# Hyena layer: the first x1 products ahead of the first convolution, half of the output rows by token halves, norms without GpSimd

## The chip, the cores and the metric

The kernel runs on one core of a Trainium2 chip. The metric is the device time of one execution in microseconds (us); lower is better. The engines are named as in the profile: PE (TensorE), DVE (VectorE), ACT (ScalarE), POOL (GpSimd) and SP (SyncE, which here only issues DMAs).

## What is computed

A trunk of two layers over 512 latent tokens of width 1024 with 256 context tokens, all in fp32. Layer 0 is attention and an MLP, layer 1 a Hyena mixer and an MLP, each behind a modulated RMSNorm. What matters here:

```python
def rmsnorm(x, g):
    y = x * lax.rsqrt(jnp.mean(x * x, axis=-1, keepdims=True) + EPS)
    return y * g

def modulate(x, g, shift, scale):
    return rmsnorm(x, g) * (1 + scale) + shift

def hyena_mixer(h, ...):
    z = short_conv(h @ w_in, conv_w, conv_b)     # 3 taps along the tokens
    x1, x2, v = jnp.split(z, 3, axis=-1)         # 1024 columns each
    y = v
    for n, gate in enumerate((x1, x2)):
        y = gate * bidir_long_conv(y, hf[:, n], hb[:, n], skip[n])   # over all 512 tokens
    return y @ w_out

x = x + g1 * hyena_mixer(modulate(x, norm1_g, sh1, sc1), ...)
x = x + g2 * sq_relu_mlp(modulate(x, norm2_g, sh2, sc2), w1, w2)
```

## The kernel before

The stream x is kept transposed as `xT`: 8 tiles of 128 features by 512 tokens. A product of near fp32 precision is made of three fp32r matmuls (`mm3`, L107): high by high, high by low, low by high. So every weight tile is split by `split_w` (L119) into `whi` (a cast on ACT) and `wlo` (a subtraction on DVE, or on POOL where `lo_eng` says so), and every operand `h` into `h_hi` and `h_lo`. Raw weights come through the two `wraw` buffers, loaded by SP; the split ones lie in two buffers `whi` and two `wlo`. PE, ACT, DVE and POOL each run their own list of instructions in order. The kernel's source gives the order in which work is stated; the Tile framework's planner makes the list of each engine from it and sets the waits.

A norm (`normT`, L409) works on one half of the tokens (256 columns). `inv_rms` (L394) squares the 8 tiles on ACT (`nsq`), lets POOL add up seven of them in `nacc` (L404), and sums over the partitions by fp32 products with ones (L405, L406). After the reciprocal root (ACT, then a Newton step on DVE) each of the 8 tiles is scaled on DVE (`nxr`, L418) and shifted to `h_hi` on ACT (L420); `h_lo` is made on DVE for even tiles (L426), and for odd ones by a second copy on ACT (L423) and a subtraction on POOL (L424). In the Hyena layer's finish these tiles lie in re-used ones, which the profile names `U` and `y`.

`project_norm_project` (L839) joins two stages by token halves A and B: the projection of half A (8 steps of 128 features), some steps of half B (`ahead`), the norm of A, the rest of B, then the first two tiles of the next product on half A, the norm of B, and those two on half B. It stands in three places: from attention to MLP 0, from MLP 0 to the Hyena layer, and from the Hyena layer to MLP 1. `add_proj_steps` (L816) makes the projection: for each pair of output tiles a weight load and split, and for each tile `kt` times `mm3` and an eviction on DVE that adds to `xT` (L835). With `kept` the split weights of half A stay for half B.

The Hyena layer (`hyena`, L1111) works on four blocks c of 256 channels. `project` (L1129) makes one of v, x1, x2 of a block in two steps, each 24 matmuls of 512 columns and the short convolution (`shorts`, L1116: three ACT evictions, four POOL additions). For each block `conv1` transposes v, makes a spectrum on PE (L948), multiplies it with a filter on DVE and prepares the inverse (`P`); `gate1` (L1168) is the inverse product on PE times x1 on DVE; then a second `hyena_conv`, whose result (`E`, `O`) goes through `gate2` (L1180) into rows 2c and 2c+1 of Y, split into `yhi` and `ylo`. Between these, `fill(n)` (L1213) takes n steps of independent products from the chain `other`, which hold PE busy while DVE works on a convolution:

```python
        other = chain(P_(0, "x1"), P_(1, "v"), P_(0, "x2"), P_(1, "x1"), P_(2, "v"), P_(1, "x2"), P_(2, "x1"), P_(3, "v"),
                      P_(2, "x2"), P_(3, "x1"), wo(0, 2), P_(3, "x2"), wo(2, 6))
        R1 = conv1(0)
        fill(4)
        for c in range(4):
            u = gate1(c, R1, turn_x1(c))
            R2 = self.hyena_conv(hp, Tf, u, load_k(1, c), False)
            if c < 3:
                R1 = conv1(c + 1)
            fill((3, 3, 3, 8)[c])
            gate2(c, R2)
            fill((3, 3, 9, 0)[c])
```

`wo(r0, r1)` is the product of rows r0 to r1-1 of Y with w_out, 8 steps (one per output tile); its low halves are made on POOL. Rows 0 to 5 are done in the loop, at 512 columns. Rows 6 and 7 are done in `finish` (L1376), by token halves through `project_norm_project`, with the split weights kept in tiles that the layer no longer needs.

Of the kernel before, what the change touches and what calls it, by code (L numbers as in the profile page):

```python
# [12 lines left out]
ALU = mybir.AluOpType  # L13
# [40 lines left out]
class Parts:  # L54


    def __init__(self, whole, rest, parts):
        self.whole, self.rest, self.turns = whole, rest, {n: cycle(i) for n, i in parts.items()}

    def tile(self, shape, dtype, name):  # L60
        if name in self.turns:
            return self.whole[:, next(self.turns[name])]
        return self.rest.tile(shape, dtype, name)


def f(ap):
    return ap.bitcast(F32)


class Kernel:  # L70
# [323 lines left out]
    def inv_rms(self, np_, cols):  # L394
# [4 lines left out]
        acc = np_.tile([P, n], F32, name="nacc")  # L399
        for k in range(KD):  # L400
            s = acc if k == 0 else np_.tile([P, n], F32, name="nsq")
            nc.scalar.activation(out=s, in_=self.xT[:, k, cols], func=AF.Square)
            if 0 < k < KD - 1:
                nc.gpsimd.tensor_tensor(out=acc, in0=acc, in1=s, op=ALU.add)  # L404
        nc.tensor.matmul(ps, self.ones, acc, start=True, stop=False)  # L405
        nc.tensor.matmul(ps, self.ones, s, start=False, stop=True)  # L406
        return self.rsqrt_bcast(np_, ps, n, 1.0 / D, "n")

    def normT(self, np_, h, gcol, shcol, cols):  # L409
# [5 lines left out]
        for k in range(KD):  # L415
# [5 lines left out]
            if k % 2:  # L421
                u = np_.tile([P, n], F32, name="nu")
                nc.scalar.activation(out=u, in_=t, func=AF.Identity, bias=sh)  # L423
                nc.gpsimd.tensor_tensor(out=lo, in0=u, in1=f(hi), op=ALU.subtract)  # L424
            else:
                nc.vector.scalar_tensor_tensor(out=lo, in0=t, scalar=sh, in1=f(hi), op0=ALU.add, op1=ALU.subtract)  # L426
# [684 lines left out]
    def hyena(self, h, zp, first, open_hp, kdram, gcol, finish):  # L1111
# [84 lines left out]
        def load_k(n, c):  # L1196
# [4 lines left out]
        wo = lambda r0, r1, cols=slice(0, S), kept=None: self.add_proj_steps(  # L1201
            w_out, list(range(r0, r1)), gcol, lambda k: Y[r0 + k], cols, kept, (nc.gpsimd, nc.gpsimd))
        Z[0] = {"v": []}
        for m in range(2):
            shorts(0, "v", 2048, m, first[m])
        hp = open_hp()
        Tf, Ti = self.load_tables(hp, True)
        P_ = lambda c, *nms: project(c, [(nm, {"v": 2048, "x1": 0, "x2": 1024}[nm]) for nm in nms])


        other = chain(P_(0, "x1"), P_(1, "v"), P_(0, "x2"), P_(1, "x1"), P_(2, "v"), P_(1, "x2"), P_(2, "x1"), P_(3, "v"),
                      P_(2, "x2"), P_(3, "x1"), wo(0, 2), P_(3, "x2"), wo(2, 6))
# [281 lines left out]
```

## Time and profile before

| | |
|---|---|
| three runs | 1565.3, 1568.7, 1571.17 us; median 1568.7 |
| the profiled execution | 1564.55 us, its span 1562.8 us |
| mean granted clock of PE | 0.976 of full speed |
| busy, share of the span | PE 93%, PE's weight loads 76%, DVE 71%, ACT 45%, POOL 26% |

Times in the trace are in us from the span's start. A matmul's row shows when it starts and how long it lasts until its result is there; matmuls overlap, so the rate of a stream is the distance of two starts, not the length of one. In brackets stands how long the engine was idle before the instruction, and what released it. The Hyena layer's first v product and the norm before it end at about 907 us, the layer's products by token halves begin at about 1167, and the MLP of layer 1 runs at full width from about 1210 to the end.

### The profile page before, as it was taken

The numbers are of one execution on the slowest core, as the hardware profiler recorded it, in microseconds if no ns is written. First come the engines' busy times: TensorE is split into PE (matmuls) and PEld (weight loads), VectorE is DVE, ScalarE is ACT, GpSimd is POOL, SyncE is SP. The second block draws the span as 40 slices with busy tenths as digits, with TensorE's granted clock in tenths as the row PEclk, the third lists the DMA queues.
The fourth block names the chain that finished last, engine by engine and source line by source line (L and its number), as shares of the span: only waits on it lengthen the run. The fifth ranks groups of instructions, "written<-read, shape, count | busy, mean of one in ns | idle before, by whom it ended". The sixth has DMA issues, their size and how long they took to land. (4 is left out here: it accounts for less than half of the span.)

```text
span 1562.8 us, 19761 instructions
## 1 busy us (share of the span) xinstructions
PE 1449.0 (93%) x7468; PEld 1192.0 (76%) x7468; DVE 1109.5 (71%) x1582; ACT 699.7 (45%) x1140; POOL 403.1 (26%) x340
## 2 busy tenths in 40 slices
PE   8688899999989999989999979999987999999998
PEld 2356588888877777878789967788776888888898
DVE  3898899887688988898765659798847434344454
ACT  3534587766653344344425444434325413232242
POOL 0440235232320322232220345445354000000001
PEclk9899999999999999999999989999998999999999
DMA  8557200221346655564334323231222223233241
GB/s 314 196 176 224 48 1 21 59 53 50 109 157 232 202 191 175 175 198 159 121 108 162 110 86 106 84 108 41 95 91 72 81 81 108 87 102 104 85 135 55
DMA packets 134461, 186.06 MB, mean 119 GB/s; under 512 B 16584, under 2 KB 117709, under 8 KB 131294
## 3 DMA queue, kind: packets, MB, share of 16 engines
q1 hardware_dynamic: 132192, 174.62, 34.6%
q0 software_dynamic: 1440, 9.70, 1.8%
q8 instruction: 59, 0.97, 0.3%
q10 hardware_dynamic: 734, 0.48, 0.1%
q14 instruction: 36, 0.29, 0.1%
HBM read 171.67 MB, written 10.49 MB: 117 GB/s over the span
## 5 line engine op out<-in xcount | busy, mean ns | idle before, releaser
L125 ACT CAST whi<-wraw 128x1024 fp32r<-128x1024 f32 (+3 forms) x211 | 198.9, 949 | 360.4 <-PE sm L110 341.1
L126 DVE TENSOR_TENSOR wlo<-wraw,whi 128x1024 fp32r<-128x1024 f32 (+2 forms) x195 | 241.4, 1242 | 105.8 <-ACT whi L125 95.8
L110 PE MATMUL sm<-h_lo,whi 128*128 128x512 f32 (+1 forms) x720 | 275.6, 384 | 3.9 <-POOL h_lo L424 3.1
L109 PE MATMUL sm<-h_hi,whi 128*128 128x512 f32 (+1 forms) x720 | 276.4, 387 | 2.2 <-ACT h_hi L420 2.2
L111 PE MATMUL sm<-h_hi,wlo 128*128 128x512 f32 (+1 forms) x720 | 274.1, 382 | 3.6 <-DVE wlo L126 3.6
L110 PE MATMUL sm<-mHlo,whi 128*128 128x512 f32 (+1 forms) x640 | 223.5, 349 | 6.0 <-DVE mHlo L172 6.0
L109 PE MATMUL sm<-mHhi,whi 128*128 128x512 f32 (+1 forms) x640 | 225.9, 353 | 0.5 <-ACT whi L125 0.3
L111 PE MATMUL sm<-mHhi,wlo 128*128 128x512 f32 (+1 forms) x640 | 223.2, 349 | 1.9 <-DVE wlo L126 1.9
L835 DVE SCALAR_TENSOR_TENSOR xT<-sm,mod,xT 128x512 f32<-128x512 f32 (+1 forms) x136 | 83.7, 621 | 150.7 <-PE sm L111 150.5
L110 PEld LDWEIGHTS sm<-h_lo,whi 128*128 128x128 f32 x720 | 136.0, 189 | 32.9 <-POOL h_lo L424 5.5
L111 PEld LDWEIGHTS sm<-h_hi,wlo 128*128 128x128 f32 x720 | 135.8, 189 | 32.1 <-DVE wlo L126 6.1
L109 PEld LDWEIGHTS sm<-h_hi,whi 128*128 128x128 f32 x720 | 134.8, 189 | 30.7 <-ACT h_hi L420 2.8
L110 PEld LDWEIGHTS sm<-mHlo,whi 128*128 128x128 f32 x640 | 121.7, 190 | 22.5 <-DVE mHlo L172 7.0
L111 PEld LDWEIGHTS sm<-mHhi,wlo 128*128 128x128 f32 x640 | 121.5, 190 | 18.7 <-DVE wlo L126 3.4
L109 PEld LDWEIGHTS sm<-mHhi,whi 128*128 128x128 f32 x640 | 121.4, 190 | 18.2 <-issue 1.7
L929 POOL TENSOR_TENSOR Kout<-kE,kO 128x512 f32<-128x512 f32 x32 | 46.3, 1471 | 264.6 <-DVE kE L1065 264.6
L370 DVE SCALAR_TENSOR_TENSOR modacc<-modw,silu,modacc 128x1024 f32<-128x1024 f32 x63 | 84.1, 1335 | 27.4 <-DMA modw<-in_w_mod 27.2
L1126 POOL TENSOR_TENSOR zx<-zx,zt 128x384 f32<-128x384 f32 x64 | 79.4, 1260 | 93.1 <-ACT zt L1124 91.8
L639 POOL TENSOR_SCALAR prob<-prob,smx 128x768 f32<-128x768 f32 x64 | 60.4, 943 | 146.9 <-DVE smx L638 91.8
L1245 POOL TENSOR_TENSOR facc<-facc,fsq 128x256 f32<-128x256 f32 x12 | 9.5, 790 | 333.1 <-ACT fsq L1243 333.1
L169 ACT CAST mHhi<-ms 128x512 fp32r<-128x512 f32 x64 | 39.6, 620 | 79.8 <-DVE ms L875 79.5
L637 ACT ACTIVATE prob<-big,smx,qry 128x768 f32<-128x768 f32 x64 | 63.7, 997 | 11.8 <-DVE smx L635 11.2
(458 smaller groups left out, 3002.4 us busy)
## 6 DMA issues: line engine op xcount, KB each, us to landing
wraw<-in_mlp_w SPq DMA_DIRECT2D x67, 1024.0 KB
modw<-in_w_mod SPq DMA_DIRECT2D x80, 512.0 KB
wraw<-in_h_w_in SPq DMA_DIRECT2D x12, 1024.0 KB
wm<-in_w_mod SPq DMA_DIRECT2D x8, 1024.0 KB
kd<-Kout POOLq DMA_DIRECT2D x8, 1024.0 KB, 5.4
Kin<-kd SPq DMA_DIRECT2D x8, 1024.0 KB
wraw<-in_a_w_in SPq DMA_DIRECT2D x5, 1024.0 KB
wraw<-in_a_w_out SPq DMA_DIRECT2D x9, 512.0 KB
```

Source lines behind the costliest of these rows:

```text
L109: mm(ps, w.hi, x.hi, start=first, stop=False)
L110: mm(ps, w.hi, x.lo, start=False, stop=False)
L111: mm(ps, w.lo, x.hi, start=False, stop=last)
L125: nc.scalar.copy(hi, r3)
L126: (lo_eng or nc.vector).tensor_tensor(out=lo, in0=r3, in1=f(hi), op=ALU.subtract)
L169: nc.scalar.copy(dst.hi, src)
L370: nc.vector.scalar_tensor_tensor(out=acc, in0=w, scalar=s, in1=acc, op0=ALU.mult, op1=ALU.add)
L637: nc.scalar.activation(out=p, in_=sf, func=AF.Exp, bias=sm[:, 1:2], scale=sc, accum_out=sm[:, 2:3])
L639: nc.gpsimd.tensor_scalar(out=p, in0=p, scalar1=sm[:, 3:4], scalar2=1.0, op0=ALU.mult, op1=ALU.mult)
L835: nc.vector.scalar_tensor_tensor(out=xt, in0=ps, scalar=gcol[:, d:d + 1], in1=xt, op0=ALU.mult, op1=ALU.add)
L929: tt = lambda e, o, x, y, op: e.tensor_tensor(out=o, in0=x, in1=y, op=op)
L1126: nc.gpsimd.tensor_tensor(out=t[:, o0:o0 + n], in0=t[:, o0:o0 + n], in1=b[:, i0:i0 + n], op=ALU.add)
```

## The change

- The two products of x1 of block 0 are stated ahead of the tables, of the first convolution and of everything else in the block loop; the chain `other` starts with v of block 1, so that each `fill` takes steps that lie one pair later.
- In the loop only rows 0 to 3 of Y go through w_out (8 steps of 12 matmuls, five ahead of x2 of block 3 and three behind it); rows 4 to 7 go through it in `finish` by token halves, with their low halves made on DVE. The `fill` counts become (3, 3, 3, 4) and (3, 3, 4, 0).
- `inv_rms` squares two tiles per ACT instruction, adds on DVE at double width, and ends in three fp32 products with ones instead of two. `h_lo` is made on DVE for all tiles; the second copy on ACT and POOL's subtraction go. This holds for all three places of `normT`.
- In `finish` the norm's tiles are laid over `U`, `E` and `O` instead of `U` alone.

```diff
--- before.py
+++ after.py
@@ -1,5 +1,5 @@
 import math
-from itertools import chain, cycle
+from itertools import chain, cycle, islice
 from contextlib import ExitStack
 
 import numpy as np
@@ -54,12 +54,12 @@
 class Parts:
 
 
-    def __init__(self, whole, rest, parts):
-        self.whole, self.rest, self.turns = whole, rest, {n: cycle(i) for n, i in parts.items()}
+    def __init__(self, rest, parts):
+        self.rest, self.turns = rest, {n: cycle(i) for n, i in parts.items()}
 
     def tile(self, shape, dtype, name):
         if name in self.turns:
-            return self.whole[:, next(self.turns[name])]
+            return next(self.turns[name])
         return self.rest.tile(shape, dtype, name)
 
 
@@ -396,14 +396,15 @@
         nc = self.nc
         n = cols.stop - cols.start
         ps = self.sm()[:, 0:n]
-        acc = np_.tile([P, n], F32, name="nacc")
-        for k in range(KD):
-            s = acc if k == 0 else np_.tile([P, n], F32, name="nsq")
-            nc.scalar.activation(out=s, in_=self.xT[:, k, cols], func=AF.Square)
-            if 0 < k < KD - 1:
-                nc.gpsimd.tensor_tensor(out=acc, in0=acc, in1=s, op=ALU.add)
-        nc.tensor.matmul(ps, self.ones, acc, start=True, stop=False)
-        nc.tensor.matmul(ps, self.ones, s, start=False, stop=True)
+        acc = np_.tile([P, 2, n], F32, name="nacc")
+        for k in range(0, KD, 2):
+            s = np_.tile([P, 2, n], F32, name="nsq") if k else acc
+            nc.scalar.activation(out=s, in_=self.xT[:, k:k + 2, cols], func=AF.Square)
+            if 0 < k < KD - 2:
+                nc.vector.tensor_tensor(out=acc, in0=acc, in1=s, op=ALU.add)
+        nc.vector.tensor_tensor(out=acc[:, 0], in0=acc[:, 0], in1=acc[:, 1], op=ALU.add)
+        for i, x in enumerate((acc[:, 0], s[:, 0], s[:, 1])):
+            nc.tensor.matmul(ps, self.ones, x, start=(i == 0), stop=(i == 2))
         return self.rsqrt_bcast(np_, ps, n, 1.0 / D, "n")
 
     def normT(self, np_, h, gcol, shcol, cols):
@@ -418,12 +419,7 @@
             nc.vector.scalar_tensor_tensor(out=t, in0=self.xT[:, k, cols], scalar=gcol[:, k:k + 1], in1=R,
                                            op0=ALU.mult, op1=ALU.mult)
             nc.scalar.activation(out=hi, in_=t, func=AF.Identity, bias=sh)
-            if k % 2:
-                u = np_.tile([P, n], F32, name="nu")
-                nc.scalar.activation(out=u, in_=t, func=AF.Identity, bias=sh)
-                nc.gpsimd.tensor_tensor(out=lo, in0=u, in1=f(hi), op=ALU.subtract)
-            else:
-                nc.vector.scalar_tensor_tensor(out=lo, in0=t, scalar=sh, in1=f(hi), op0=ALU.add, op1=ALU.subtract)
+            nc.vector.scalar_tensor_tensor(out=lo, in0=t, scalar=sh, in1=f(hi), op0=ALU.add, op1=ALU.subtract)
 
     def new_h(self, hp):
         return Split(hp.tile([P, KD, S], F32R, name="h_hi"), hp.tile([P, KD, S], F32R, name="h_lo"))
@@ -1198,18 +1194,22 @@
             nc.sync.dma_start(out=K, in_=kdram[n][c])
             return K
 
-        wo = lambda r0, r1, cols=slice(0, S), kept=None: self.add_proj_steps(
-            w_out, list(range(r0, r1)), gcol, lambda k: Y[r0 + k], cols, kept, (nc.gpsimd, nc.gpsimd))
+        wo = lambda r0, r1, lo_eng, cols=slice(0, S), kept=None: self.add_proj_steps(
+            w_out, list(range(r0, r1)), gcol, lambda k: Y[r0 + k], cols, kept, (lo_eng, lo_eng))
         Z[0] = {"v": []}
         for m in range(2):
             shorts(0, "v", 2048, m, first[m])
+        P_ = lambda c, *nms: project(c, [(nm, {"v": 2048, "x1": 0, "x2": 1024}[nm]) for nm in nms])
+
+        for _ in P_(0, "x1"):
+            pass
         hp = open_hp()
         Tf, Ti = self.load_tables(hp, True)
-        P_ = lambda c, *nms: project(c, [(nm, {"v": 2048, "x1": 0, "x2": 1024}[nm]) for nm in nms])
-
-
-        other = chain(P_(0, "x1"), P_(1, "v"), P_(0, "x2"), P_(1, "x1"), P_(2, "v"), P_(1, "x2"), P_(2, "x1"), P_(3, "v"),
-                      P_(2, "x2"), P_(3, "x1"), wo(0, 2), P_(3, "x2"), wo(2, 6))
+
+
+        out = wo(0, 4, nc.gpsimd)
+        other = chain(P_(1, "v"), P_(0, "x2"), P_(1, "x1"), P_(2, "v"), P_(1, "x2"), P_(2, "x1"), P_(3, "v"),
+                      P_(2, "x2"), P_(3, "x1"), islice(out, 5), P_(3, "x2"), out)
         fill = lambda n: [next(other, None) for _ in range(n)]
         R1 = conv1(0)
         fill(4)
@@ -1218,14 +1218,14 @@
             R2 = self.hyena_conv(hp, Tf, u, load_k(1, c), False)
             if c < 3:
                 R1 = conv1(c + 1)
-            fill((3, 3, 3, 8)[c])
+            fill((3, 3, 3, 4)[c])
             gate2(c, R2)
-            fill((3, 3, 9, 0)[c])
+            fill((3, 3, 4, 0)[c])
         fill(99)
         kept = [Alias(p, {"whi": (hi, b), "wlo": (lo, b)}) for p, hi, lo, b in (
             (zp, "zv", "zx1", 2), (zp, "zv", "zx1", 2), (hp, "fcb", "fsb", 1), (zp, "zx2", "zx2", 2),
             (hp, "P0", "P1", 1), (hp, "kw0", "kw1", 1), (hp, "kw2", "kw3", 1), (hp, "ft0", "ft1", 1))]
-        return finish(lambda hf: wo(6, 8, hf, kept))
+        return finish(lambda hf: wo(4, 8, nc.vector, hf, kept))
 
 
     def final(self, fp, hf):
@@ -1375,9 +1375,10 @@
 
             def finish(proj):
                 h = self.new_h(hp)
-                np_ = Parts(hy[0].tile([P, 8, 256], F32, name="U", bufs=1),
-                            Alias(hy[0], {"nxr": ("y1", 3), "nu": ("y1", 3)}),
-                            {"nacc": (0, 1), "ny": (2, 3), "nv": (4, 5), "nt": (6,), "nsq": (7, 6)})
+                U, E, O = (hy[0].tile([P, n, 256], F32, name=nm, bufs=1) for nm, n in (("U", 8), ("E", 4), ("O", 4)))
+                np_ = Parts(Alias(hy[0], {"nxr": ("y1", 3)}),
+                            {"nacc": (U[:, 0:2], U[:, 2:4]), "nsq": (U[:, 4:6], U[:, 6:8]), "ny": (E[:, 0], E[:, 1]),
+                             "nv": (E[:, 2], E[:, 3]), "nt": (O[:, 0], O[:, 1])})
                 wx = (Alias(hy[0], {"whi": ("u", 2), "wlo": ("u", 2)}),
                       Alias(hy[0], {"whi": ("x1T", 1), "wlo": ("Kin", 1)}))
                 return h, self.project_norm_project(
```

## Rows read from the trace of the kernel before

**Rows 1.** Busy time by stage; us, busy (instructions) by engine, PEclk, DMA share, GB/s.
```profile
910.00:920.00 10.00, 6.03 (x17) 4.49 (x18) 0.00 (x0) 3.13 (x5) 4.13 (x7) 0.54 0.01 2
...
949.00:1004.00 55.00, 52.63 (x242) 43.81 (x241) 47.07 (x55) 22.12 (x33) 25.71 (x23) 1.00 0.29 96
...
1059.00:1118.00 59.00, 54.53 (x244) 45.10 (x242) 52.61 (x60) 21.00 (x36) 27.86 (x28) 0.97 0.24 81
...
1167.00:1211.00 44.00, 32.55 (x202) 29.32 (x203) 32.26 (x55) 21.62 (x47) 18.08 (x21) 0.88 0.31 96
```

**Rows 2.** Timeline of PE, opening; start, length, engine, line, operation, count, [idle before <-releaser].
```profile
907.14 0.28 PE L111 MATMUL sm<-h_hi,wlo 128*128 128x256 f32 x1
...
913.98 1.54 PE L1151 MATMUL sm<-cst,zv 128*128 128x128 f32 x6 [2.11 <-POOL zv L1126]
...
916.20 6.14 PE L948 MATMUL sm<-u,Tf 128*128 128x256 f32 x16 [0.68 <-ACT u L1159]
...
921.99 0.58 PE L109 MATMUL sm<-h_hi,whi 128*128 128x512 f32 x1
```

**Rows 3.** Timeline of ACT at the opening.
```profile
891.82 1.05 ACT L125 CAST whi<-wraw 128x1024 fp32r<-128x1024 f32 x1 [1.52 <-PE sm L110]
...
914.92 1.23 ACT L1159 COPY u<-sm 128x512 f32<-128x512 f32 x2 [2.71 <-PE sm L1151]
...
927.63 1.06 ACT L125 CAST whi<-wraw 128x1024 fp32r<-128x1024 f32 x1 [5.52 <-PE sm L110]
```

**Rows 4.** Timeline of DVE: first convolution, block 2, block 3.
```profile
920.07 1.29 DVE L941 TENSOR_TENSOR ft<-sm,fcb 128x512 f32<-128x512 f32 x2 [14.81 <-PE sm L948]
...
947.03 1.48 DVE L1081 TENSOR_TENSOR P<-O 128x512 f32<-128x512 f32 x1
...
1059.93 1.29 DVE L1177 TENSOR_TENSOR u<-sm,x1T 128x512 f32<-128x512 f32 x2 [1.99 <-ACT x1T L1165]
...
1103.88 2.12 DVE L1081 TENSOR_TENSOR P<-O 128x512 f32<-128x512 f32 x2
...
1118.19 1.28 DVE L1177 TENSOR_TENSOR u<-sm,x1T 128x512 f32<-128x512 f32 x2
...
1139.13 2.10 DVE L1081 TENSOR_TENSOR O<-U 128x512 f32<-128x512 f32 x2
```

**Rows 5.** Timeline of PE, w_out inside the loop.
```profile
1143.72 0.50 PE L111 MATMUL sm<-yhi,wlo 128*128 128x512 f32 x1 [2.52 <-POOL wlo L126]
```

**Rows 6.** Timeline of PE from the end of w_out in the loop to the MLP.
```profile
1154.10 0.39 PE L111 MATMUL sm<-yhi,wlo 128*128 128x512 f32 x1
...
1154.33 1.89 PE L1187 MATMUL sm<-Ti,E 128*128 128x256 f32 x8
...
1166.69 0.28 PE L109 MATMUL sm<-yhi,zv 128*128 128x256 f32 x1
...
1172.74 0.28 PE L111 MATMUL sm<-yhi,kw 128*128 128x256 f32 x1
...
1175.62 0.28 PE L111 MATMUL sm<-yhi,fsb 128*128 128x256 f32 x1
...
1181.39 1.22 PE L405 MATMUL sm<-U,ones 128*128 128x256 f32 x2 [5.49 <-POOL U L404]
...
1210.49 0.40 PE L109 MATMUL sm<-h_hi,whi 128*128 128x512 f32 x1
```

**Rows 7.** Timeline of DVE in the norm ahead of the Hyena layer, second half.
```profile
897.85 0.88 DVE L418 SCALAR_TENSOR_TENSOR nxr<-xT,mod,ny 128x256 f32<-128x256 f32 x2
...
900.72 0.47 DVE L426 SCALAR_TENSOR_TENSOR h_lo<-nxr,mod,h_hi 128x256 fp32r<-128x256 f32 x1
...
901.22 1.61 DVE L418 SCALAR_TENSOR_TENSOR nxr<-xT,mod,ny 128x256 f32<-128x256 f32 x2
```

**Rows 8.** Groups by line and shape; count | busy us, mean ns | idle before.
```profile
L126 DVE TENSOR_TENSOR wlo<-wraw,whi 128x512 fp32r<-128x512 f32 x18 | 12.6, 712 | 0.7 <-ACT whi L125 0.7
...
L126 POOL TENSOR_TENSOR wlo<-wraw,whi 128x512 fp32r<-128x512 f32 x8 | 10.5, 1318 | 21.1 <-ACT whi L125 21.1
```

## What the change does to the time, worked out before it was run

> **What bounds the kernel now.** I read the page first: TensorE (PE) is busy 93% of the span, VectorE (DVE) 71%. A PE at 93% hides its idle time in a few stages, so I then took busy time by stage over the Hyena layer and, inside it, the timelines of PE, ScalarE (ACT), DVE and GpSimd (POOL). Three places stand out.
>
> The opening: PE issues its last product of the v columns at 907.14 and its first x1 product at 921.99 [rows 2]; the 14.9 us between hold 8 transposes and 16 spectrum matmuls. The transposes wait for the short convolution that POOL adds up (2.11 us are shown before the later six), and the granted clock from 910 to 920 is 0.54 of full speed, most of it at the lower level (1.2 GHz), so the 16 spectrum matmuls take 6.14 us [rows 1, 2]. DVE starts its first convolution at 920.07 after 14.81 us idle [rows 4].
>
> The block loop: one block takes 55 us, in which DVE is busy 47 [rows 1]: PE decides, with DVE 8 us behind it.
>
> The end: PE stands three times in the loop for a low half of w_out that POOL makes, 2.52 us in the instance shown [rows 5], and then 5.49 us for POOL's sums of squares; the stretch after that is at a granted clock below 1, which over the whole finish is 0.88 on average [rows 1, 6]. From the first token-half product (1166.69) to the first full-width MLP product (1210.49) pass 43.8 us [rows 6].
>
> Two prices are used throughout. 46 matmuls of 512 columns start between 1143.72 and 1154.10 [rows 5, 6], 0.23 us each; 25 of 256 columns start between 1172.74 and 1175.62 [rows 6], 0.12 us each. A block of x1, x2 or v is 48 of the former: 11.0 us. A step of w_out with four rows of Y is 12 matmuls, 2.8 us at full width and 1.44 us at half width.
>
> **Opening.** The x1 products of block 0 move ahead of the first convolution. Their weights need no wait: the cast that ends at 892.9 is the last of the two that precede them [rows 3]. So PE goes on at 907.3 and is through with x1 at 918.3, by when the v columns are long added. Then come 8 transposes (1 us). What is late next is ACT, which runs its list in order: it has the cast of the next weights (1.06 us, as at 927.63 [rows 3]), three evictions of x1 (2.1 us, each a little above the 0.62 us of a copy of u of the same width; bounds 0 if the copies go first, 3.5 with a wait for POOL's buffers) and the two copies of u (1.23 us [rows 3]). I take 4.4 us after 918.3, so spectra start near 922.5. At full clock 16 of them take 3.7 us instead of 6.1 (fp32 pairs at 0.22 us; the 16 convolution products from 1154.33 take 2 x 1.7 [rows 6]), so PE reaches the v products of block 1 at 926, having done x1, which it now finishes at 933. That is -7 us for PE (bounds -4 to -9). DVE, however, starts its chain near 924 in place of 920.07, 4 us later. The SP queue is not disturbed: tables and K are issued behind the same weight loads, and the zx, zv tiles lie in a pool that is open already. POOL gets the x1 additions before those of v(1) as now.
>
> **Block loop.** Since the products run one pair of steps ahead, PE reaches gate 1 of block 0 with x2(0) done as well. It gets there at 926 + 4 x 5.5 + 1 = 949; its last quarter needs DVE's last P, which ends at 948.5 now [rows 4] and near 951.5 then (27.3 us of chain from 924, the 1.1 us wait for the slow spectrum gone). So gate 1 is over near 952, 2.5 us later than now, with 11 us more products behind it. Blocks 0 and 1 keep their fills (3 and 3 steps), so their 55 us stay. In block 2 the fill shrinks from 3 + 9 steps (32.6 us) to 2 x1 steps and 5 w_out steps (25 us): PE needs some 44 us, DVE took 46.1 from 1059.93 to 1106.0 [rows 4], and now two y multiplications, low halves and w_out evictions (0.7 us each) fall into that chain, +2 net of two weight splits that go earlier. DVE decides: its last P comes at 1062.4 + 48 = 1110.4, and u at 1111.5 instead of 1118.19 [rows 4]. In block 3 the fill goes from 8 steps (27 us plus the POOL wait) to 4 (16.6 us), so gate 2 waits for DVE: 23.0 us from u to the end of O now (1118.19 to 1141.23 [rows 4]) plus one weight split, 1.2. Gate 2 then starts at 1135.7, against 1154.33 [rows 6]. With its 6.9 us and one w_out step the token-half products start at 1145.4, against 1166.69: **-21.3 us** (bounds -12, DVE late by its 4 us throughout, and -27, no DVE lateness from block 2 on). PE's waits for POOL's low halves are taken as gone: between the first and second w_out step now lies gate 2, and in the steady steps from 1144 on there is none.
>
> One oddity: the fifth w_out step leaves a weight pair half used while x2(3) asks for the same two buffers, so half of x2(3) comes after the sixth step. Its split (1.05 + 1.2 us) has 2.8 us of w_out to hide behind; uncovered it costs 2 us.
>
> **End.** Half of Y's rows (4 to 7) instead of a quarter go by halves. 48 matmuls of 512 columns (11.0 us) leave the loop, counted above, and 96 of 256 (11.5 us) come here: +0.5 us for the width. Weights: 4 loads of 512 KB through two buffers with 8 casts and 8 low halves, now on DVE. POOL takes 1.3 us for such a tile, DVE 0.7 [rows 8]. A pair is due every 2.9 us, and DVE's 1.4 us lies in time when it waits for gate 2; bounds 0 and 5.5 us, I take 0. Gain: 4 steps of the B half (5.8 us) now stand where 2.9 us stood before the norm's row sums, and the sums come from DVE: the 5.49 us wait [rows 6] goes, and with it the slow clock, about 2.5 us. PE is then late on DVE's h of the A half (4 us by my count of DVE's list: 16 norm operations at 0.47, five evictions, splits of MLP weights) and in the B half runs at DVE's pace. Sum for the finish: 43.8 + 11.5 - 5.5 - 2.5 - 2 (smaller waits) = 45.3 (bounds 41 and 50): **+1.5 us**.
>
> **Norms.** Six halves (three layers). Each loses six POOL additions, four POOL h_lo and four ACT copies; DVE gains four h_lo (0.47 [rows 7]), two double-width adds (0.7, as the tile of that width in [rows 8]) and one of 256 (0.4): 3.7 us; PE gains one fp32 product, two passes of 0.22, 0.43 us. Against that, DVE runs its first factor in 0.44 us when POOL is still and two of them in 1.61 when POOL works beside it [rows 7]: some four operations a half pay 0.5 us, and in the stretches where the adds, splits and evictions meet POOL about as much again. Net DVE 0 (bounds -1 and +3.7). At the first two norms PE has products to cover the sums, so only the fp32 product remains: **+0.9 us** for four halves, half of it hidden (bounds -3 and +15).
>
> **Width, by the skill.** The Trainium skill (Perfetto Trace Analysis, Optimizing Tensor Performance, Matmuls) says larger matmuls are the more efficient ones; the move to 256 columns goes against it. The trace gives the price above, 2 x 0.12 for 0.23: half a microsecond in all, so the sum stays whichever one goes by.
>
> **How the numbers follow.** -21.3 + 1.5 + 0.9 = -19 us. The profiled execution took 1564.55 us (span 1562.8), 4 us under the median of the three runs, 1568.7. I carry the difference to the median: 1568.7 - 19.5 = **1549**.
>
> **Rivals.**
> - *DVE bounds the loop from the start.* For: DVE has 47 of 55 us [rows 1] and starts 4 us late. Then gate 2 of block 3 starts at 1145 and the finish at 1155: -12 + 2.5 = -9.5, 1559. Against: in blocks 0 and 1 DVE has idle time to catch up. Chance 0.18.
> - *The order isn't what the source says.* Tile's planner puts each engine's list in order by its own estimates; if the transposes and the first convolution go ahead of x1, the opening stays and its -7 is lost: 1556. Chance 0.08.
> - *Better than forecast.* The planner fills PE's waits for DVE with later products, the finish comes to 41: -28, 1541. Chance 0.14.
> - *Slower: DVE bounds the norms.* All it takes over is on the path: 4.1 us in each of six halves (25 us) and 5.5 us of low halves in the finish, while the finish keeps its 11.5 us: with -21 from the loop and -5.5 for the sums, +15, 1584. It decides where DVE is without a gap through a half, and at half its price, with the loop's gain at its lower bound, it is still +9. For: DVE is busy 32 of 44 us in the finish now [rows 1]. Against: POOL's going gives DVE back what the rows show [rows 7]. Chance 0.08. The Trainium skill (Perfetto Trace Analysis, Optimizing Scalar/DVE Operations) speaks for this rival: where DVE is saturated, work may go from it to Scalar or even GPSIMD, the opposite of this change; it adds that the two share a read port, so that this might not help. The factors' rows [rows 7] bear out the second half here.
> - *Gains and losses cancel*, within 0.5% (1561 to 1576.5; that is about what a measurement of this kernel tells from no change): the loop at its lower bound with the norms at +5 to +12. Chance 0.13.
>
> Forecast itself (1544 to 1556): 0.39. Faster by over 0.5%: 0.39 + 0.18 + 0.08 + 0.14 = 0.79; same 0.13; slower 0.08. The range leaves out the slower case and a tenth at the ends: 1535 to 1566.
>
> **What would show it.** PE timeline: x1 products directly behind the v products, no gap of 10 us near 910, clock 1.0 there, DVE's first convolution 3 to 4 us later than 920. Blocks of 55, 55, 48 us, gate 2 of block 3 near 1136 and waiting for DVE. No PE wait for POOL's wlo or sums; first full-width MLP product near 1190. Before 907 hardly a difference. Wrong it would be if the first norm (before 451) were longer by several microseconds, if PE's waits for wlo reappeared with DVE as releaser, or if a block took more than 57.

## The result, and the profile after

The change takes 1545.8 us where the kernel before takes 1567.1 us; the ratio is 0.987 (95% interval 0.984 to 0.990). A second series, on the chip of the last experiments, gave 1548.4 against 1567.0 (0.9885, interval 0.9866 to 0.9904). 1549 was forecast. The profiled span went from 1562.8 to 1541.4 us.

The page after, its first part (busy us, share of the span, instructions by engine). PE is busy as long as before (1449.0), with 60 instructions more; POOL lost a sixth of its busy time (403.1 before).

```profile
PE 1448.1 (94%) x7528; PEld 1196.3 (78%) x7528; DVE 1107.9 (72%) x1624; ACT 683.2 (44%) x1084; POOL 337.9 (22%) x264
```

PE's timeline after: the opening, then from the last gate 1 to the finish (start, length, engine, line, operation, count, [idle before <-releaser]).

```profile
901.69 0.40 PE L109 MATMUL sm<-h_hi,whi 128*128 128x512 f32 x1
...
911.01 1.04 PE L1147 MATMUL sm<-cst,zv 128*128 128x128 f32 x8
914.87 5.21 PE L944 MATMUL sm<-u,Tf 128*128 128x256 f32 x16 [2.82 <-ACT u L1155]
919.73 0.58 PE L109 MATMUL sm<-h_hi,whi 128*128 128x512 f32 x1
...
1107.70 5.41 PE L944 MATMUL sm<-u,Tf 128*128 128x256 f32 x16 [2.31 <-DVE u L1173]
...
1129.82 0.50 PE L111 MATMUL sm<-yhi,wlo 128*128 128x512 f32 x1 [1.32 <-POOL wlo L126]
...
1132.26 1.89 PE L1183 MATMUL sm<-Ti,E 128*128 128x256 f32 x8
...
1141.93 0.28 PE L109 MATMUL sm<-yhi,zv 128*128 128x256 f32 x1
...
1146.56 0.56 PE L109 MATMUL sm<-yhi,zv 128*128 128x256 f32 x1 [2.03 <-ACT yhi L169]
...
1162.33 1.46 PE L407 MATMUL sm<-U,ones 128*128 128x256 f32 x6
...
1176.21 1.86 PE L407 MATMUL sm<-U,ones 128*128 128x256 f32 x6 [2.37 <-DVE U L405]
...
1188.45 0.40 PE L111 MATMUL sm<-h_hi,wlo 128*128 128x512 f32 x1
```

Beside [rows 2]: the x1 products now run up to the transposes, which no longer wait for POOL's zv; the spectra wait for ACT instead. Beside [rows 5, 6]: the token-half products start at 1141.93 instead of 1166.69, one wait for a low half of POOL is left (1.32), and the 5.49 us wait ahead of the A half's row sums is gone (1162.33). Three waits are new: 2.31 for DVE's u, 2.03 for ACT's yhi, and 2.37 for DVE's sums of the B half, ahead of which PE did not wait before.

**Stages.** Execution against execution, times drift in stages that nothing touched: the first stage alone, up to 408.8 us before, took 408.8 to 418.7 us in the profiles of this study. So kernels are compared by stages, each the difference between the starts of two named PE instructions in the timeline. N1: last matmuls of the attention to the products behind the first norm. M: a stretch of the first MLP 25 us later. N2: the second norm up to its last sum. Op: from there to the first gate 1 (L1175 before, L1171 after). B0, B1: one block each. B23: third gate 1 to the first token-half product. F: from there to the last half-width product of the MLP. E: last full-width product to the end of PE's last matmul. us:

```
                      N1     M     N2     Op     B0     B1     B23     F      E
before               48.75  24.47  12.26  49.63  56.17  55.03  110.65  43.69  51.79
n_norms_only         47.82  19.87  11.59  47.68  57.81  55.07  111.22  43.95  51.94
a_opening_only       48.44  21.31  12.25  54.15  57.83  55.05  101.03  42.30  51.77
ab_old_norms         49.07  22.39  12.24  54.38  56.16  55.06   86.43  47.77  53.78
bc_old_opening       46.95  19.98  11.59  47.59  57.80  55.05   94.52  45.50  52.94
the change           47.15  20.07  11.60  52.23  57.85  55.01   86.50  46.40  53.34
change_again         47.93  19.96  11.59  52.26  57.80  55.03   86.46  46.80  53.52
hlo_on_pool          47.93  22.69  12.42  52.71  56.25  55.07   86.40  46.20  52.98
sums_on_pool         46.82  19.65  12.27  52.22  57.87  54.99   86.47  46.12  51.91
fin_lo_on_pool       45.71  19.89  11.60  52.24  57.82  55.07   90.80  47.45  53.00
cover_one_step       47.40  19.85  11.60  50.77  56.13  55.05   86.38  44.07  53.93
v0_on_dve            47.52  19.91  11.59  50.78  56.16  55.00   86.42  44.45  54.14
v0_first             46.88  19.83  11.59  57.67  54.32  55.05   84.75  45.49  55.42
v0_first_cover       47.90  19.89  11.59  57.67  54.34  54.98   84.76  43.89  53.08
```

From before to the change: N1 -1.6, M -4.4, N2 -0.7, Op +2.6 (with 11 us more of products in it), B0 +1.7, B23 -24.2, F +2.7, E +1.6; with +0.9 net in the stretches left out, -21.4 of the span.

The longest stretch left out, some 376 us from M to N2, holds the filter stage and takes 372.9 to 380.2 us in these profiles. before, a_opening_only and ab_old_norms run the same lists of instructions up to N2, and take 376.4, 380.0 and 374.1 us for it. So a gain of 1 to 3 us ahead of it can't be followed to the end of the kernel.

**The clock.** Several of these stages take two values some 1.5 to 2 us apart, and the kernel doesn't decide which. Five stretches of the change, each behind a wait of PE of 0.9 to 3 us (us, busy by engine, PEclk, DMA share, GB/s):

```profile
914.60:919.60 5.00, 4.73 (x15) 3.96 (x16) 1.14 (x2) 1.14 (x3) 1.51 (x3) 0.67 0.60 206
946.00:954.00 8.00, 6.83 (x25) 5.41 (x26) 4.32 (x7) 1.17 (x2) 2.78 (x3) 0.79 0.39 131
1106.00:1114.00 8.00, 6.30 (x21) 5.21 (x22) 4.32 (x7) 1.17 (x2) 0.00 (x0) 0.79 0.00 0
1145.00:1153.00 8.00, 6.44 (x41) 6.44 (x42) 4.37 (x8) 2.18 (x5) 0.00 (x0) 0.79 0.43 133
1175.00:1183.00 8.00, 6.79 (x37) 6.44 (x38) 5.40 (x13) 2.40 (x5) 0.00 (x0) 0.79 0.00 1
```

And the same five in the run v0_on_dve, whose waits there are as long (2.82, 0.86, 2.31, 2.16, 2.37 us):

```profile
922.40:927.40 5.00, 4.83 (x22) 4.20 (x23) 2.29 (x5) 1.29 (x3) 1.42 (x3) 1.00 0.59 204
952.00:960.00 8.00, 5.89 (x29) 4.74 (x30) 6.00 (x10) 2.25 (x4) 3.00 (x3) 1.00 0.39 131
1108.00:1116.00 8.00, 5.69 (x19) 4.45 (x19) 5.14 (x8) 0.58 (x1) 0.00 (x0) 0.80 0.00 0
1148.00:1156.00 8.00, 5.84 (x47) 5.44 (x46) 5.33 (x11) 2.29 (x4) 0.00 (x0) 1.00 0.42 121
1177.00:1185.00 8.00, 5.17 (x36) 4.61 (x34) 5.60 (x14) 2.80 (x6) 0.00 (x0) 1.00 0.00 1
```

A granted clock below 1 is a part of the stretch at 1.2 instead of 2.4 GHz. Sixteen spectrum matmuls whose start lies at the lower level take 5.41 us (1107.70 above), all at the upper 3.72: 1.7 us. The second comes from cover_one_step, which runs the same lists as the change up to block 3:

```profile
920.39 3.72 PE L944 MATMUL sm<-u,Tf 128*128 128x256 f32 x16 [2.83 <-ACT u L1155]
```

In the profile of the change all five fell, in that of v0_on_dve one. A stage that differs by 1.5 to 2 us together with its granted clock is therefore not the kernel's: in Op 52.2 and 50.8 are one value, in B0 57.8 and 56.2, in F 46.4 and 44.5. M has such a pair too. It is at 1.00 in all kernels but before and hlo_on_pool (the stretches M of before, the change and hlo_on_pool):

```profile
482.11:506.58 24.47, 20.93 (x90) 16.72 (x89) 22.16 (x29) 9.22 (x15) 0.00 (x0) 0.93 0.70 231
480.84:500.90 20.06, 18.75 (x90) 15.49 (x89) 18.40 (x24) 8.47 (x14) 0.00 (x0) 1.00 0.74 245
487.80:510.50 22.70, 20.64 (x91) 16.90 (x90) 20.29 (x26) 9.33 (x15) 0.00 (x0) 0.92 0.70 230
```

### The profile page after: what moved, and what is told of

Its sections match the earlier page's. It is cut to its first block, busy times and chain, and to the rows that moved or that the text cites. A ratio compares the mean times of both kernels' runs of the same rounds, so it can differ in the third digit from the quotient of the medians.

```text
span 1541.4 us, 19704 instructions
## 1 busy us (share of the span) xinstructions
PE 1448.1 (94%) x7528; PEld 1196.3 (78%) x7528; DVE 1107.9 (72%) x1624; ACT 683.2 (44%) x1084; POOL 337.9 (22%) x264
## 5 line engine op out<-in xcount | busy, mean ns | idle before, releaser
L125 ACT CAST whi<-wraw 128x1024 fp32r<-128x1024 f32 (+2 forms) x203 | 195.7, 970 | 340.3 <-PE sm L110 316.6
L126 DVE TENSOR_TENSOR wlo<-wraw,whi 128x1024 fp32r<-128x1024 f32 (+2 forms) x195 | 234.5, 1206 | 115.5 <-ACT whi L125 101.9
L831 DVE SCALAR_TENSOR_TENSOR xT<-sm,mod,xT 128x256 f32<-128x256 f32 (+1 forms) x128 | 78.0, 613 | 132.2 <-PE sm L111 132.0
L110 PEld LDWEIGHTS sm<-h_lo,whi 128*128 128x128 f32 x720 | 136.2, 189 | 28.1 <-DVE h_lo L422 1.6
L1122 POOL TENSOR_TENSOR zx<-zx,zt 128x384 f32<-128x384 f32 x64 | 64.4, 1027 | 60.5 <-ACT zt L1120 59.2
```

Of the source, the lines that this page charges most:

```text
L110: mm(ps, w.hi, x.lo, start=False, stop=False)
L125: nc.scalar.copy(hi, r3)
L126: (lo_eng or nc.vector).tensor_tensor(out=lo, in0=r3, in1=f(hi), op=ALU.subtract)
L831: nc.vector.scalar_tensor_tensor(out=xt, in0=ps, scalar=gcol[:, d:d + 1], in1=xt, op0=ALU.mult, op1=ALU.add)
L1122: nc.gpsimd.tensor_tensor(out=t[:, o0:o0 + n], in0=t[:, o0:o0 + n], in1=b[:, i0:i0 + n], op=ALU.add)
```

## The experiments

The three parts are called A (opening), B (w_out: half of its rows by halves, and the shorter fills) and C (norms). The theory is that of the forecast; each expectation names its rival.

### n_norms_only: C alone

```diff
 before.py with inv_rms, normT, Parts and the finish's tiles of after.py; nothing else
```

> The kernel before with the new norms alone (old opening, old end: a quarter of the rows by halves, low halves on POOL). Theory of the forecast: at the first two norms PE has products to cover the sums, so the four halves cost +0.9 us, and in the finish DVE's sums take 2 to 4 us off the 5.49 us wait: 1563 to 1566 us beside 1567. Rival, from the two traces: with POOL quiet DVE and ACT hand over the halves of h sooner than PE asks for them, the first two norms gain 4 to 5 us, and with the finish the whole is -7 to -9: 1558 to 1560.

1564.8 against 1569.2 us (0.9973, interval 0.9951 to 0.9995). Neither was right as a whole: -4.3 us lies beyond the theory's -1 to -4 and short of the rival's -7 to -9. M and N2 fall as the rival said, Op by 2.0, but F stays (43.69 and 43.95, both at a mean clock of 0.88): the finish alone gains nothing from the norm. PE waits ahead of the A half's row sums as long for DVE as it did for POOL (5.49):

```profile
1183.88 2.93 PE L407 MATMUL sm<-U,ones 128*128 128x256 f32 x6 [5.85 <-DVE U L405]
```

### a_opening_only: A alone

```diff
+        for _ in P_(0, "x1"):
+            pass
         hp = open_hp()
-        other = chain(P_(0, "x1"), P_(1, "v"), P_(0, "x2"), ...
+        other = chain(P_(1, "v"), P_(0, "x2"), ...
-            fill((3, 3, 3, 8)[c])
+            fill((3, 3, 3, 6)[c])
```

> The kernel before with the x1 products of block 0 stated first and the pairs shifted by one; w_out, norms and the number of steps left behind the last gate as before. Theory of the forecast: PE bounds the long fills, so its 6 to 7 us of the opening arrive whole at the finish: 1560 to 1561 us. Rival: DVE starts its first convolution about 4 us later and sets gate 1 of each block; then no more than 2 to 3 us arrive: 1564 to 1565.

1563.1 against 1569.2 us (0.9953, interval 0.9931 to 0.9976), -6 us. Op grows by 4.5 us, with 11 us of products more in it: the opening gains 6.5. Of the 11 us B23 gives back 9.6. So the theory holds here; it lost 1.4 us of the 6.5 on the way.

### ab_old_norms: the change without C

```diff
-        acc = np_.tile([P, 2, n], F32, name="nacc")
+        acc = np_.tile([P, n], F32, name="nacc")      (inv_rms and normT as before,
...                                                     laid over U, E and O)
```

> The changed kernel with the old norms (squares one by one, sums and every other h_lo on POOL), laid over U, E and O as in the change; low halves of the finish stay on DVE. Theory of the forecast: the first two norms differ by less than 1 us, the finish loses 2 to 4 us at POOL's sums: 1547 to 1550 against 1546 for the change. Rival: 4 to 5 us come back at the first two norms and 4 to 6 in the finish, where two halves of the sums are on POOL: 1554 to 1557.

1551.8 us against 1569.2 for before, -17.4 where the two series of the change have -21.2 and -18.7: C is worth 1.3 to 3.8 us by whole times, less than its 4.3 alone, and the two intervals (0.986 to 0.991 here) overlap. By stages the change is shorter by 1.9 (N1), 2.3 (M), 0.6 (N2), 2.1 (Op) and 1.4 (F), 8.3 us. Of that the stretch from M to N2 takes back 3.7 in these two profiles, and the better clock that this run's profile had in B0 another 1.7.

### bc_old_opening: the change without A

```diff
-        for _ in P_(0, "x1"):
-            pass
-        other = chain(P_(1, "v"), P_(0, "x2"), ...
+        other = chain(P_(0, "x1"), P_(1, "v"), P_(0, "x2"), ...
-            fill((3, 3, 4, 0)[c])
+            fill((3, 3, 6, 0)[c])
```

> The changed kernel with the old opening: the x1 products of block 0 behind the first convolution's spectra, one pair later in the list, so that each block ends with the same product as in the change. Theory of the forecast: the parts add, the opening's 6 to 7 us come back: 1552 to 1553 us. Rival: with the short fills of blocks 2 and 3 DVE sets the end, and DVE starts some 4 us earlier with the old opening: 1546 to 1549, next to nothing lost.

1552.3 us, -16.9 against its own before: 1.8 to 4.3 less than the change. By stages A costs 4.6 in Op and gives back 8.0 in B23, where it gave 9.6 without B: 3.4 net, about half way between theory and rival. What takes the rest is a wait that the change has and this run has not: in block 3 the spectra wait 2.31 us for DVE's u and then run at the lower clock (1107.70 above). Here only a low half of POOL holds PE in that stretch, 1.70 us:

```profile
1105.66 0.50 PE L111 MATMUL sm<-yhi,wlo 128*128 128x512 f32 x1 [1.70 <-POOL wlo L126]
```

With the shorter fill DVE sets block 2, and part of A's lead is spent waiting for it.

No run has B alone. From the pairs of this series, bc_old_opening less n_norms_only and ab_old_norms less a_opening_only, it is worth 12.6 and 11.3 us, the largest of the three parts.

### hlo_on_pool and sums_on_pool: the two halves of C

```diff
 hlo_on_pool: every other h_lo on POOL, from a copy u that ACT makes
+            if k % 2:
+                u = np_.tile([P, n], F32, name="nu")
+                nc.scalar.activation(out=u, in_=t, func=AF.Identity, bias=sh)
+                nc.gpsimd.tensor_tensor(out=lo, in0=u, in1=f(hi), op=ALU.subtract)
 sums_on_pool: six additions on POOL, squares one by one, two products with ones
+            if 0 < k < KD - 1:
+                nc.gpsimd.tensor_tensor(out=acc, in0=acc, in1=s, op=ALU.add)
```

> The changed kernel with every other h_lo of the norms on POOL again (with ACT's extra copy for it), the sums of squares staying with DVE. The old norms as a whole cost 6 to 7 us against the change (1551.8 to 1545.8; profiled spans 1548.4 to 1541.4). If the halves of h make that (PE waits for POOL's h_lo at the products behind each norm), 4 to 6 us come back: 1550 to 1552. If the sums make it, 0 to 2: 1546 to 1548.

> The changed kernel with the sums of squares as before (squares one by one on ACT, six additions on POOL, two products with ones), every h_lo staying on DVE. If the sums make the 6 to 7 us of the norms (the finish waits for POOL's additions), 4 to 6 come back: 1550 to 1552 us. If the halves of h make it, 0 to 2: 1546 to 1548. If neither run gives back more than 2, it is the two together, POOL beside DVE.

1553.4 us (its four times lie between 1547 and 1559, so alone it says little) and 1547.2 us. By stages more shows: with the h_lo on POOL, N2 goes from 11.6 to 12.4 and Op, whose clock was at the upper level in that run, from 50.8 to 52.7; F, at the upper clock too, is 46.2 beside 44.5 (v0_on_dve). M goes from 19.9 to 22.7, but at a clock of 0.92 instead of 1.00, which by the figures above makes some 1.7 us of it (an estimate: 0.075 of 22.7). With the sums on POOL only N2 moves (0.7), and F is as in the change at the same lower clock, 46.1 and 46.4. Groups by line and shape, PE's products on h_lo in the norm's halves and DVE's factor (count | busy us, mean ns | idle before, releaser). Before:

```profile
L110 PE MATMUL sm<-h_lo,whi 128*128 128x256 f32 x64 | 19.1, 307 | 3.9 <-POOL h_lo L424 3.1 <-DVE h_lo L426 0.6
...
L418 DVE SCALAR_TENSOR_TENSOR nxr<-xT,mod,ny 128x256 f32<-128x256 f32 x32 | 20.9, 683 | 0.7
```

The change:

```profile
L110 PE MATMUL sm<-h_lo,whi 128*128 128x256 f32 x64 | 18.6, 295 | 0.9 <-DVE h_lo L422 0.9
...
L419 DVE SCALAR_TENSOR_TENSOR nxr<-xT,mod,ny 128x256 f32<-128x256 f32 x32 | 14.0, 479 | 0.1
```

hlo_on_pool:

```profile
L110 PE MATMUL sm<-h_lo,whi 128*128 128x256 f32 x64 | 19.2, 304 | 3.6 <-POOL h_lo L425 3.2 <-DVE h_lo L427 0.3
...
L419 DVE SCALAR_TENSOR_TENSOR nxr<-xT,mod,ny 128x256 f32<-128x256 f32 x32 | 20.7, 675 | 0.7
```

sums_on_pool:

```profile
L110 PE MATMUL sm<-h_lo,whi 128*128 128x256 f32 x64 | 18.5, 301 | 0.4 <-DVE h_lo L421 0.4
...
L418 DVE SCALAR_TENSOR_TENSOR nxr<-xT,mod,ny 128x256 f32<-128x256 f32 x32 | 15.4, 523 | 0.1
```

POOL's h_lo costs twice: PE waits 3.2 us for it, in pieces of 0.3 to 0.6, and it takes DVE's factor from 479 to 675 ns. The sums on POOL cost 0.7 us in N2 and lengthen a few factors (523 ns in the mean). The Trainium skill (SBUF — State Buffer, Who interferes with whom) says that a DVE instruction with two inputs in SBUF contends with a GpSimd instruction that reads SBUF; the factor has two such inputs, and the rows agree.

### fin_lo_on_pool: the kept weights' low halves on POOL

```diff
-        return finish(lambda hf: wo(4, 8, nc.vector, hf, kept))
+        return finish(lambda hf: wo(4, 8, nc.gpsimd, hf, kept))
```

> The changed kernel with the low halves of the finish's kept weights on POOL instead of DVE (8 tiles at 1.3 us instead of 0.7). Theory: DVE is the engine that sets the finish, so giving it 5.5 us less work helps or costs nothing: 1543 to 1546 us. Rival: a pair is due every 2.9 us and POOL needs 2.6 us for one, so the first pairs come late and PE waits again for POOL's low halves: 1549 to 1552.

1553.0 us against 1568.6 for before (0.9894, interval 0.9862 to 0.9927), -15.7: 3 to 5.5 us less than the change. The rival's size, but not its place: F is 1 us longer, B23 4.3. The wait stands ahead of the last gate 2, in the loop (PE, then POOL):

```profile
1137.42 0.58 PE L111 MATMUL sm<-yhi,wlo 128*128 128x512 f32 x1 [4.08 <-POOL wlo L126]
```

```profile
1132.03 3.67 POOL L126 TENSOR_TENSOR zx<-wraw,zv 128x512 fp32r<-128x512 f32 x2
1135.66 1.71 POOL L126 TENSOR_TENSOR wlo<-wraw,whi 128x512 fp32r<-128x512 f32 x1
```

POOL makes the two kept low halves (zx) first, and the one that PE needs at once behind them, 3.67 us later: POOL's list has them in this order.

### cover_one_step: more work behind the last gate

```diff
-            fill((3, 3, 3, 4)[c])
+            fill((3, 3, 3, 3)[c])
```

> The changed kernel with one w_out step of the loop moved from ahead of the last second gate to behind it (the fill of block 3 is 3 steps instead of 4; same work). Theory: the 2.03 us wait for ACT's yhi behind the first half-width products and the half clock after it (about 1.7 us) come from too little work between the last gate and the halves; with 2.8 us more there, PE waits 1.3 us less at POOL's low half ahead of the gate too: 2 to 4 us faster, 1542 to 1544 us. Rival: the y halves of ACT stand behind casts of kept weights that wait for their transfers (2.44 us), so the wait only moves: 1545 to 1547.

1546.4 us (0.9862, interval 0.9822 to 0.9902), no difference that can be told from the change. The rival was right: B23 is the same within 0.1, F 44.07 beside 44.45 at the same (upper) clock, and PE still waits 1.53 us for ACT's yhi. Ahead of the gate POOL's 1.32 us are gone as the theory said, but PE waits 0.82 and 0.33 us there for DVE's E and O instead:

```profile
1131.17 1.97 PE L1183 MATMUL sm<-Ti,E 128*128 128x256 f32 x8 [0.82 <-DVE E L1077]
...
1148.78 0.38 PE L109 MATMUL sm<-yhi,zv 128*128 128x256 f32 x1 [1.53 <-ACT yhi L169]
```

ACT's timeline in the change tells why yhi is late:

```profile
1140.76 1.66 ACT L169 CAST yhi<-y 128x512 fp32r<-128x512 f32 x3
1144.86 0.62 ACT L125 CAST kw<-wraw 128x512 fp32r<-128x512 f32 x1 [2.44 <-DMA wraw<-in_h_w_out]
1145.38 0.61 ACT L125 CAST ft<-wraw 128x512 fp32r<-128x512 f32 x1
1145.90 0.61 ACT L169 CAST yhi<-y 128x512 fp32r<-128x512 f32 x1
```

The last yhi, which PE needs at 1144.5, stands behind the casts of two kept weights, and the first of these waits 2.44 us for its transfer.

### change_again, v0_on_dve, v0_first, v0_first_cover: does DVE's start decide?

```diff
 v0_on_dve: block 0's v columns are added up by DVE
-                    nc.gpsimd.tensor_tensor(out=t[:, o0:o0 + n], ...
+                    (nc.vector if c == 0 and nm == "v" else nc.gpsimd).tensor_tensor(out=t[:, o0:o0 + n], ...
 v0_first: that, and
-        R1 = conv1(0)
+        with self.tc.high_priority(offset=500):
+            R1 = conv1(0)
 v0_first_cover: that, and fill((3, 3, 3, 3)[c])
```

> The changed kernel as it is, beside the next three on the same chip: 1544 to 1548 us, and a second profile, which shows how far stages that no part touches (the first 200 us, the filter stage to 860) differ from one execution to the next.

> The changed kernel with the short convolution of block 0's v columns (8 additions) on DVE, which is idle there, instead of POOL; nothing stated in another order. Theory: PE's order stays (x1 products, then transposes, then spectra), zv is ready earlier but nobody asks for it, ACT's copies of u stay behind its evictions: within 1 us of the change, spectra still 3.9 us behind the first transpose. Rival: what holds the spectra is POOL and zv; then the first spectrum comes 2 us sooner.

> The same with the first convolution given priority in the planner's list: 8 transposes among the first x1 products, spectra ahead of the last of them, DVE's chain starting 5 to 6 us sooner relative to the end of the norm; the same work. Theory that DVE's chain sets the end from block 2 on: 3 to 5 us faster than the change, 1541 to 1543 us, even if PE waits 1 to 3 us in the opening. Rival, PE sets the blocks: what PE waits in the opening is lost, 1547 to 1549.

> The same with one w_out step moved behind the last second gate (as in the run with cover). Theory: the two add, 2 us more: 1539 to 1541 us. Rival: with DVE sooner the gate no longer waits, and the step behind it gives nothing: as the run before.

1548.4, 1543.9, 1549.2 and 1545.8 us. change_again repeats every stage from Op to B23 within 0.1 us, while the first stage took 2.5 us more.

v0_on_dve: zv is added up sooner, and PE's wait ahead of the spectra is the same 2.82 us: it is for ACT's copies. Op, B0 and F are shorter than in the change by 1.5, 1.7 and 2.0, and each time the granted clock differs (the fences above). Its time (0.985, interval 0.983 to 0.987) overlaps that of change_again by a hair; a gain is not shown, and no stage has one that isn't the clock's.

v0_first: the first spectrum comes 6.7 us sooner behind the norm, and the first gate 1 5.4 us later. The priority put the convolution's operations on DVE ahead of a weight split that PE needed; the cast for it ended at 931.53, and DVE came to it at 937.47, after five operations of the convolution of which one was running (ACT, DVE, PE):

```profile
930.48 1.05 ACT L125 CAST whi<-wraw 128x1024 fp32r<-128x1024 f32 x1 [2.00 <-PE sm L110]
937.47 1.43 DVE L126 TENSOR_TENSOR wlo<-wraw,whi 128x1024 fp32r<-128x1024 f32 x1
938.95 0.79 PE L111 MATMUL sm<-h_hi,wlo 128*128 128x512 f32 x1 [5.98 <-DVE wlo L126]
```

Op to B23 sum to 251.8 us, as in the change (251.6); but v0_on_dve, which met the upper clock in Op and B0, takes 248.4, so the wait and the lower clock behind it (0.64 over the next 8 us) cost more than DVE's lead brought. Block 2 takes PE 46.2 us from gate 1 to gate 1 in every kernel with A and B, whenever DVE started in block 0. So the run can't say what an earlier start alone would bring; but that block 2 is as long with it and PE waits for u as before speaks against the theory. What fits all of these runs is that DVE's length in block 2 decides, not its start in block 0.

## Why the prediction was right, and where not

**Total.** -19 was forecast, -18.7 and -21.2 measured. By terms errors cancel, and that the total is so near is luck: the norms alone brought 4.3 us (n_norms_only; interval 0.8 to 7.7) where +0.9 was forecast, opening and loop brought 1 to 2 less, and finish and E together cost 3 more. (The terms add up to -18.9; the forecast then takes off 19.5.) The clock did not decide it: both profiled executions have a mean of 0.976.

**Opening, -7 for PE.** a_opening_only: -6.5. The first spectrum came 24.5 us behind the norm's last sum; at the upper clock 16 of them take 3.72, as forecast, but in the change they met 0.67 and took 5.21. DVE's first convolution starts 3.3 us later against that sum (28.1 and 24.9 us; 4 was forecast). The wait that I expected behind it, ACT's list, is the one that came: 2.82 us.

**Loop, -21.3.** Op to B23: -20.2 between n_norms_only and the change, whose norms and clock in B0 are alike, and -19.4 between before and ab_old_norms. Block 2 was forecast at 48 us for PE and DVE; it is 46.2 between PE's gates and 47.7 from u to u on DVE:

```profile
1059.28 1.29 DVE L1173 TENSOR_TENSOR u<-sm,x1T 128x512 f32<-128x512 f32 x2 [1.98 <-ACT x1T L1161]
...
1106.96 1.28 DVE L1173 TENSOR_TENSOR u<-sm,x1T 128x512 f32<-128x512 f32 x2
```

From 1063.86 to the second of these rows DVE has no gap over 0.15 us. It decides there, as said, but PE's 2.31 us wait for u and the 1.7 us of lower clock behind it had no term. Block 0 took 57.85 us, above the 57 that was named as a sign of being wrong; at the upper clock it is 56.2 (v0_on_dve), so the clock made that. Gate 2 of block 3 was forecast to wait for DVE; it starts at 1132.26, which against the norm's last sum (-4.9 us) is 1.4 us later than forecast, behind the one low half of POOL (1.32 us) whose wait I had declared gone. The step "in the steady steps there is none" failed. It was not POOL's queue: POOL stood idle for ACT's cast, and the cast for PE's last product of x2 of block 3, which held the weight buffer (ACT, POOL):

```profile
1127.09 0.62 ACT L125 CAST whi<-wraw 128x512 fp32r<-128x512 f32 x1 [0.83 <-PE sm L110]
1127.79 1.98 POOL L126 TENSOR_TENSOR wlo<-wraw,whi 128x512 fp32r<-128x512 f32 x1 [0.57 <-ACT whi L125]
```

The forecast's "oddity" has this collision over the two buffers, but only for the weights of x2. DVE was close behind: where POOL's wait is gone (cover_one_step), PE waits 0.82 us for DVE's E at this gate.

**Finish, 45.3.** 46.4, and 44.5 where the clock stayed up (v0_on_dve). PE's waits over the finish sum to 11.4 us before (1167 to 1211) and 4.4 in the change (1142 to 1189), so of the 11.5 us of products that came here 7 fill what was idle. The 5.49 us wait ahead of the A half's sums went, as forecast. Of the two causes that the forecast gives, the runs show one: with DVE's sums and the old end (n_norms_only) PE waits 5.85 us there, with POOL's sums and the new end (ab_old_norms, sums_on_pool) not at all. It is the new end, whose four steps of the B half ahead of those sums are twice as long (5.8 us for 2.9 in the forecast); DVE in POOL's place did nothing there. What the forecast had no term for is the wait ahead of the B half's sums, 2.37 us for DVE in the change and 2.07 for POOL in sums_on_pool. Two stretches at the lower clock, which I took as gone with the sums' wait, stand in the change behind this wait and behind that for ACT's yhi. The latter is one that I didn't list: I named the queues that the kept weights' low halves move past, not that of their casts.

**Norms, +0.9 for four halves.** This is the step that failed: "at the first two norms PE has products to cover the sums, so only the fp32 product remains". The sums are covered, but the halves of h are not. In the trace before, PE stands three times 0.34 us for POOL's h_lo in the second norm and six times in the first, and [rows 7] show DVE's factor doubled; the forecast credited that to DVE and nothing to PE. hlo_on_pool measures it at the same clock: 1.9 in Op (against v0_on_dve), 0.8 in N2; ab_old_norms adds some 1 to 2 us in N1. In M, 25 us behind the norm, 1.7 of the 4.4 us between before and the change are the clock (an estimate: 0.07 of 24.47), the rest PE's waits, mostly for DVE's low halves (3.5 us before, 1.3 after). At 1.00 M takes 21.31 and 22.39 with the old norms (a_opening_only, ab_old_norms) and 19.65 to 20.07 with all h_lo on DVE. Why it depends on the norm at all is not settled; the planner lists DVE's operations there in another order. How much of N1 and M reaches the end is open as well, for the stretch to N2 scatters by more.

**End of the kernel.** E is 1 us or more longer in nearly all kernels with B (52.9 to 55.4 against 51.8 to 51.9), but 51.91 in sums_on_pool. In the change PE waits 1.17 us for ACT's mHhi there. No run explains it.

**Rivals.** That DVE bounds the loop came true for block 2 alone and leaves A half of its gain (3.4 of 6.5); 1.7 us of the loss are the clock behind the wait for u. The slower case, DVE without a gap in the norms, did not come: with POOL gone DVE's factors and low halves became shorter (683 to 479 and 572 to 480 ns). The 32 factors of the first two norms take 6.9 us less of DVE's time, and the 16 low halves that it took over there cost 7.7: nearly even.

## What to carry to other kernels

Work that a second engine takes off a busy one can cost more than it saves if it slows the first beside it and the engine behind both waits for the slower half: add up repeated waits of 0.3 us with the same releaser by group. Ahead of moving work forward in a list, ask which in-order queue stands behind its loads and casts, not only behind its arithmetic. And compare variants by stages of one engine's timeline, with the granted clock of each stage beside it: at the same clock Op to B23 repeat to 0.1 us here where whole times scatter by 10. But add the stages up again, and hold the sum against the whole: what one stage gains, a stretch that isn't in the table can take back.

## What the runs showed of the hardware

After the same wait the granted clock falls in one execution and not in the next. PE's first spectrum behind 2.82 us of idle time met a clock of 0.67 (the change) and 1.00 (v0_on_dve) over the next 5 us; behind 0.86 us in block 0 it met 0.79 and 1.00 over 8 us. cover_one_step, whose lists are those of the change up to block 3, met 1.00 both times. A fall costs 1.7 us on sixteen 256-column fp32 products, and four of them stand between the profiles of the change and of v0_on_dve: 5.1 us over Op, B0 and F, as much as a whole part of this change.

DVE's factor, which reads two inputs of 128x256 from SBUF, took 0.47 to 0.48 us in all 32 instances of the first two norms in the change, which leaves POOL out of them, up to 0.97 us with POOL's sums beside it (sums_on_pool) and up to 1.06 with POOL's h_lo (before, hlo_on_pool).
